# A hybrid state-space, attention and retrieval layer: part of the sorting, the state transposes and the value projection put at other places in the program

## The chip, the cores and the metric

The kernel runs on one core of a Trainium2 chip. The metric is device time of one execution in microseconds (us). Before the change, three timed runs gave 998.7 us as their median (997.2 to 999.82). TensorE multiplies (PE in the profile, its weight loads PEld), VectorE is DVE, ScalarE is ACT, GpSimd is POOL, SyncE (SP) issues the DMAs.

## The reference

One decoder layer over 256 tokens of 1024 numbers. Cut to what matters here:

```
proj = h @ w_in                                  # u | q | k | v, 512 columns each
y_ssm = _s5(u, ...)                              # 32 groups of a diagonal complex state, scan, GELU, GLU
y_att = _moba(q, k, v)                           # 8 heads of 64, causal over one block of 256
h = _layernorm(DN_ALPHA * h + concat([y_ssm, y_att]) @ w_out, ...)
# then the retrieval, per token:
q = (h @ w_q).reshape(tokens, 8 heads, 2, 128)
s = einsum('thcd,hcnd->thcn', q, sub_keys)       # 16 score lists of 128 for a token
s1, i1 = top_k(s[:, :, 0], 16); s2, i2 = top_k(s[:, :, 1], 16)
cand = s1[..., :, None] + s2[..., None, :]       # best 16 of them: eidx, softmax g
out = einsum(g * gelu(h . expert_u[eidx]), expert_v[eidx])
```

## The kernel before, in words

Almost all products are made of float32 matrices split into a high and a low part: ScalarE casts `hi`, VectorE (sometimes GpSimd) subtracts to get `lo`, and TensorE runs three passes (xh times hi, xl times hi, xh times lo). The retrieval is computed densely: all 16384 expert rows are streamed through and the gates are multiplied in.

A scheduler fixes one order of instructions for each engine when the program is built. It works from the order in which the code is written and from what depends on what; `tc.issue_after(x)` keeps what a block issues on x's engine behind x. On the chip each engine follows its list, so an instruction that waits holds all that stands behind it.

**The mixer** is written as steps named in `CFG['order']`, run by `do(w)`. The steps that matter: `u`, `q`, `k`, `v` are the four projections (`tokproj`, line 162, and `chproj`, line 173; 16 or 32 products each, and each float32 product is two MATMULs in the trace). `b` makes the state matrix `Bbd` on VectorE. `min` (`s5_min`, line 346) transposes it on TensorE in 32 products, and ScalarE copies them to `MinT`. `e0` and `e1` (line 410) multiply U by MinT, 64 columns wide. `s0`, `s1` are the scans on VectorE. `a0` and `a1` are four attention steps each (`attend`): scores of two heads (line 517: 64 rows, 128 columns, and line 521, the mask), row maximum on VectorE, exponential on ScalarE, transposes of the result (line 531). `kin` (line 392), `p0`, `p1`, `o0`, `o1` and `glu` close the mixer.

PSUM banks come from three pools: `w` with four (pw in the trace), `s` with two (psb), `a` with two (pa). `e0` takes both banks of `s`, `e1` both of `a`; the value projection uses `s`, the transposed probabilities use `a`.

**The routing**: `w_q` comes as 16 matrices `hc`. The first four are done together; hc = 4 to 15 are loaded and split one by one (line 826 and 828; with hc % 4 == 3 the subtraction is on GpSimd) and multiplied by `dense`. `scores(hc, ..)` makes for each of the two token halves b one list of 128 scores (line 812, 813), 32 lists in all, and while hc < EARLY (16 before) `top16` sorts it at once on VectorE: MAX, MAX_INDEX, MATCH_REPLACE, MAX, MAX_INDEX (lines 801 to 805). Three of these five are two instructions in the trace. The rest of the routing, `route(b)`, is a generator of steps; the main loop over 64 rows of `expert_u` (pairs, `u_pair`, u0 to u63; each `lo` is line 79) takes STEPS steps of it in its first PAIRS pairs. In `route(b)` ScalarE expands the indices `topi[b]` of all 16 lists of its half (`fv`, line 896).

Of the kernel before, what the change touches and what calls it, by code (L numbers as in the profile page):

```python
# [15 lines left out]
OP = mybir.AluOpType  # L16
# [25 lines left out]
def f32(ap):  # L42
    return ap.bitcast(F32)


CFG = dict(order='mask zero u par b min q rt rot k e0 e1 s0 a0 a0 a0 a0 s1 a1 a1 a1 a1 v c0 c kin p0 o0 p1 o1 glu',
           glu='VV',
           post='VV',
           yt='AAAAVVVVVVVPVVVV',
# [4 lines left out]
def layer(ctx, tc, I, out, tap=None, upto=None):  # L54
    nc = tc.nc
    V, S, P, PE = nc.vector, nc.scalar, nc.gpsimd, nc.tensor
# [45 lines left out]
    def sbank(shape):  # L102
        return ps.tile(shape, F32, tag="s", bufs=2, name="psb")
# [6 lines left out]
    with ExitStack() as px:  # L110
# [6 lines left out]
        with ExitStack() as mx:  # L117
# [5 lines left out]
            def eng(g, i):  # L123
                return P if CFG[g][i] == "P" else V

            prm = se.tile([128, 1088], F32, name="prm")
            xT = const.tile([128, ND, T], F32, tag="xh", name="xT")
# [25 lines left out]
            Uv = U.rearrange("p a b c -> p a (b c)")  # L153
            qk = sb.tile([128, 2, 4, T], F32, name="qk")

            def tokproj(blk, pt):
                for q in range(4):
                    w = w_in(blk, q)
                    for k in range(2):
                        d = 2 * q + k  # L160
                        for b in range(2):
                            PE.matmul(pt[b], xT[:, d, 128 * b:128 * b + 128],  # L162
                                      w[:, 512 * k:512 * k + 512], start=d == 0, stop=d == 7)

            def chproj(blk, scale):
                pt = [pbank([128, 2, T])[:, 0] for _ in range(4)]
                for q in range(4):
                    w = w_in(blk, q)
                    for k in range(2):
                        d = 2 * q + k  # L170
                        for m in range(4):
                            c = slice(512 * k + 128 * m, 512 * k + 128 * m + 128)
                            PE.matmul(pt[m], w[:, c], xT[:, d], start=d == 0, stop=d == 7)  # L173
                for m in range(4):
                    S.activation(qk[:, blk - 1, m], pt[m], AF.Copy, scale=scale)


            pw = sb.tile([128, 40, NPAIR], F32, name="pw")
# [117 lines left out]
            rot = sb.tile([128, 2, NPAIR, NCH], F32, name="rot")  # L296
# [44 lines left out]
            def s5_min():  # L341
                for ri in range(2):
                    for a in range(4):
                        pt = sbank([128, 4, 128])
                        for i in range(4):
                            PE.transpose(pt[:, i], Bbd[:, ri, 4 * a + i].rearrange("p j g -> p (j g)"),
                                         ident)
                        S.copy(MinT[:, ri, 4 * a:4 * a + 4], pt)
# [65 lines left out]
            def s5_scan(h, e, Sst):  # L414
# [13 lines left out]
                zr, zi = b4[1][:, sl], b4[3][:, sl]  # L428
                E = CFG["post"][h]
                V.tensor_tensor(b4[0][:, sl], zr, c_, op=OP.mult)  # L430
# [9 lines left out]
            def s5_out(h, Sst, yT):  # L440
# [10 lines left out]
                for j in range(4):  # L451
                    for q in range(4):
                        o, i = (yT[32 * q:32 * q + 32, 2 * h:2 * h + 2, :, j, :],
                                Y[32 * j:32 * j + 32, 2 * h:2 * h + 2, q])
                        e = CFG["yt"][4 * j + q]
                        S.copy(o, i) if e == "A" else (P if e == "P" else V).tensor_copy(o, i)
# [99 lines left out]
            M = {}  # L556
            zx = sb.tile([128, 2, NPAIR, NCH], F32, tag="zx", name="zx") if "P" in CFG["post"] else None

            def do(w):
                if w == "zero":  # L560
                    V.memset(Bbd, 0.0)
                    P.memset(Cbd, 0.0)
                    P.memset(Rt[:, :, 0:1], 0.0)
                    S.activation(Kin, ident[:, None, :].to_broadcast([128, NPAIR, 128]), AF.Copy,
                                 scale=0.0)
                elif w == "u":
                    pu = [abank([128, 512]) for _ in range(2)]
                    tokproj(0, pu)
                    for b in range(2):
                        V.transpose(U[:, :, b, :], pu[b].rearrange("p (a g) -> p a g", g=32))  # L570
                elif w == "q":
                    chproj(1, 0.125)
                elif w == "k":
                    chproj(2, 1.0)
                elif w == "v":
                    pv = [sbank([128, 512]) for _ in range(2)]
                    tokproj(3, pv)
                    M["v"] = vn = sb.tile([128, 2, 512], F32, tag="vn", name="vn")
                    for b in range(2):
                        S.copy(vn[:, b], pv[b])  # L580
                elif w == "par":
                    M["p"] = s5_params()
                elif w == "b":
                    s5_b(M["p"][0])
                elif w == "c0":
                    s5_c0()
                elif w == "c":
                    s5_c()
                elif w == "rt":
                    s5_rt(M["p"][1])  # L590
                elif w == "rot":
                    s5_rot()
                elif w == "min":
                    s5_min()
                elif w == "kin":
                    s5_kin()
                elif w in ("e0", "e1"):
                    M[w] = s5_e(int(w[1]))
                elif w in ("s0", "s1"):
                    if "S" not in M:  # L600
                        M["S"] = sb.tile([128, 2, NPAIR, NCH + 1], F32, tag="MinT", name="Sst")
                        P.memset(M["S"][:, :, :, 0:1], 0.0)
                    s5_scan(int(w[1]), M["e" + w[1]], M["S"])
                elif w in ("o0", "o1"):
                    if "y" not in M:
                        M["y"] = se.tile([128, 4, 2, 4, 32], F32, tag="yT", name="yT")
                    s5_out(int(w[1]), M["S"], M["y"])
                elif w == "mask":
                    masks()
                elif w in ("a0", "a1"):  # L610
                    if w not in M:
                        M[w] = attend(int(w[1]))
                    next(M[w])
                elif w in ("p0", "p1"):
                    values(int(w[1]), M["v"])
                elif w == "glu":
                    glu(M["y"])
                else:
                    raise ValueError(w)

            for w in CFG["order"].split():
                do(w)
# [14 lines left out]
            po = [[pbank([128, 512]) for _ in range(2)] for _ in range(2)]  # L637
            LATE = CFG["late"]
            W3 = sb.tile([128, 4, 1024], F32R, tag="MinT", name="W3")
# [79 lines left out]
            for q in range(4):  # L719
                raw = stream.tile([128, 1024], F32, tag="raw", bufs=RAWB, name="raw")  # L720
                for k in range(2):
                    c = 256 * q + 128 * k
# [3 lines left out]
                if q < 2:  # L726
                    r = late.tile([128, 2, 1024], F32R, tag="W4", bufs=2, name="W4")
                    hi, lo = r[:, 0], r[:, 1]
                else:
                    hi, lo = (stream.tile([128, 1024], F32R, tag=t, bufs=n, name=t)  # L730
                              for t, n in (("hi", HIB), ("lo", LOB)))
# [61 lines left out]
    with ExitStack() as rx:  # L793
# [10 lines left out]
            V.max(vals[:, 8:16], tmp)  # L804
            V.max_index(idx[:, 8:16], vals[:, 8:16], tmp)

        EARLY = 16

        def scores(hc, qT):
            for b in range(2):  # L810
# [7 lines left out]
        for hc in range(4, 16):  # L818
            raw = load(I["w_q"][hc])
            if hc == 4:  # L820
                with tc.issue_after(w4dma.ins):
                    nc.sync.dma_start(keys, I["keys"])
            hi, lo = (stream.tile([128, 1024], F32R, tag=t, bufs=n, name=t)
                      for t, n in (("hi", HIB), ("lo", LOB)))
            with tc.issue_after(cast.ins) if hc == 4 else ExitStack():
                S.copy(hi, raw)
            with tc.issue_after(normed.ins) if hc == 4 else ExitStack():
                (P if hc % 4 == 3 else V).tensor_tensor(lo, raw, f32(hi), op=OP.subtract)
            pt = abank([128, 2, T])[:, 0]
            dense(PE, pt, hi, lo, xh, xl)  # L830
            qT = sb.tile([128, T], F32, tag="qT", bufs=2, name="qT")
            S.copy(qT, pt)
            scores(*todo.pop(0))
            if len(todo) > 1:
                scores(*todo.pop(0))
            todo.append((hc, qT))
# [99 lines left out]


        steps, last = chain(route(0), route(1)), weigh()
        STEPS, PAIRS, GAP = 36, 26, 2
        done = 0  # L940
        for n in range(HALF // 2):
            low, ac = u_pair(2 * n)
# [25 lines left out]
    with tc.tile_pool(name="gk", bufs=1) as gk:  # L968
# [38 lines left out]
        for n in range(HALF // 2):  # L1007
# [3 lines left out]
            m = GT * made  # L1011
            made = due
            pt = sbank([128, 2, T])
            for r in range(2):
                hi, lo = split(load(I["u"][HALF + 2 * n + r]), P if r else V)
# [7 lines left out]
            raw = gk.tile([128, 2, T], F32, tag="ga", bufs=2, name="ga")  # L1023
# [5 lines left out]
        for i, t in enumerate(("o1", "o1", "eq")):  # L1029
            w = gk.tile([128, 2, T], F32R, tag=t, bufs=2 if t == "o1" else 1, name="wg")  # L1030
# [160 lines left out]
```

## Time and profile before

| | |
|---|---|
| median of 3 timed runs | 998.7 us (997.2 to 999.82) |
| the profiled execution: its own time, its span | 999.71 us, 997.9 us |
| PE busy | 965.8 us, 97% of the span |
| PEld, DVE busy | 855.0 us (86%), 714.9 us (72%) |
| ACT, POOL busy | 459.0 us (46%), 161.5 us (16%) |
| mean granted TensorE clock | 0.988 |
| chain that ended last | PE 81%, DVE 17%, issue 1% |

A busy share is an average over stages. TensorE is busy almost throughout; what it still waits for is read stage by stage, from the idle time ahead of its rows, and from the granted clock: 1.00 is full speed (2.4 GHz), 0.50 half of it (1.2 GHz), and at half speed TensorE counts as busy all the same.

### The profile page before, as it was taken

The numbers are of one execution on the slowest core, as the hardware profiler recorded it, in microseconds if no ns is written. First come the engines' busy times: TensorE is split into PE (matmuls) and PEld (weight loads), VectorE is DVE, ScalarE is ACT, GpSimd is POOL, SyncE is SP. The second block draws the span as 40 slices with busy tenths as digits, with TensorE's granted clock in tenths as the row PEclk, the third lists the DMA queues.
The fourth block names the chain that finished last, engine by engine and source line by source line (L and its number), as shares of the span: only waits on it lengthen the run. The fifth ranks groups of instructions, "written<-read, shape, count | busy, mean of one in ns | idle before, by whom it ended". The sixth has DMA issues, their size and how long they took to land.

```text
span 997.9 us, 16315 instructions
## 1 busy us (share of the span) xinstructions
PE 965.8 (97%) x6286; PEld 855.0 (86%) x6286; DVE 714.9 (72%) x1396; ACT 459.0 (46%) x737; POOL 161.5 (16%) x92
## 2 busy tenths in 40 slices
PE   7899999999999999999999999999999999999995
PEld 3785977989999999999999988888888888888884
DVE  8955477997766755988789999755555555555556
ACT  3224454545454445454444334544555454455552
POOL 2000003100000000354556565500000000000002
PEclk9889999999999999999999999999999999999998
DMA  8311284436555666355443434656566686666661
GB/s 326 117 43 43 82 256 134 143 126 194 186 186 177 188 185 178 124 151 154 143 151 123 130 125 148 212 184 195 190 193 190 197 274 198 193 190 193 191 198 51
DMA packets 49789, 166.24 MB, mean 167 GB/s; under 512 B 5296, under 2 KB 9392, under 8 KB 49584
## 3 DMA queue, kind: packets, MB, share of 16 engines
q1 hardware_dynamic: 49712, 165.20, 52.6%
q8 instruction: 49, 0.80, 0.3%
q14 instruction: 28, 0.23, 0.1%
HBM read 163.09 MB, written 2.10 MB: 166 GB/s over the span
## 4 chain that ended last, share of the span: by engine, by line
PE 81%; DVE 17%; issue 1%; ACT 0%; DVEq 0%
PE pw L1041 35%; PE psb L1111 29%; PE pa L1111 3%; PE pw L173 3%; DVE lo L72 2%; DVE o L984 2%; DVE act L996 2%; PE pw L989 2%; PE pw L646 2%; PE psb L162 2%; DVE o L981 1%; PE pw L517 1%; DVE eq L982 1%; PE pw L392 1%; PE psb L446 1%
## 5 line engine op out<-in xcount | busy, mean ns | idle before, releaser
L72 DVE TENSOR_TENSOR lo<-raw,hi 128x1024 fp32r<-128x1024 f32 x163 | 211.3, 1296 | 152.8 <-ACT hi L71 148.3
L71 ACT CAST hi<-raw 128x1024 fp32r<-128x1024 f32 x195 | 206.1, 1057 | 200.1 <-PE pw L1041 166.4
L1111 PE MATMUL psb<-xh,lo 128*128 128x256 f32 x1024 | 152.6, 289 | 6.5 <-DVE lo L79 4.3
L1111 PE MATMUL psb<-xh,hi 128*128 128x256 f32 x1024 | 158.1, 291 | 0.4 <-ACT act L848 0.4
L1111 PE MATMUL psb<-xl,hi 128*128 128x256 f32 x1024 | 153.7, 289 | 0.0
L1041 PE MATMUL pw<-hi,wh 128*128 128x512 f32 x492 | 151.9, 389 | 1.0 <-ACT wh L961 1.0
L1041 PE MATMUL pw<-hi,wl 128*128 128x512 f32 x492 | 152.1, 390 | 0.1
L1041 PE MATMUL pw<-lo,wh 128*128 128x512 f32 x492 | 151.8, 389 | 0.0
L1111 PEld LDWEIGHTS psb<-xh,lo 128*128 128x128 f32 x1024 | 133.9, 192 | 7.3 <-DVE lo L79 4.5
L1111 PEld LDWEIGHTS psb<-xh,hi 128*128 128x128 f32 x1024 | 135.5, 192 | 2.3 <-issue 1.0
L1111 PEld LDWEIGHTS psb<-xl,hi 128*128 128x128 f32 x1024 | 132.9, 191 | 0.0
L79 DVE TENSOR_TENSOR lo<-raw,hi 128x1024 fp32r<-128x1024 f32 x64 | 78.1, 1221 | 57.1 <-ACT hi L78 57.1
L72 POOL TENSOR_TENSOR lo<-raw,hi 128x1024 fp32r<-128x1024 f32 x32 | 83.0, 2592 | 218.0 <-ACT hi L71 202.5
L1041 PEld LDWEIGHTS pw<-hi,wh 128*128 128x128 f32 x492 | 92.3, 188 | 20.5 <-ACT wh L961 1.4
L1041 PEld LDWEIGHTS pw<-hi,wl 128*128 128x128 f32 x492 | 92.2, 188 | 20.1 <-DVE wl L962 1.0
L1041 PEld LDWEIGHTS pw<-lo,wh 128*128 128x128 f32 x492 | 92.4, 188 | 19.1
L78 ACT CAST hi<-raw 128x1024 fp32r<-128x1024 f32 x64 | 66.9, 1047 | 89.5 <-PE psb L1111 81.3
L996 DVE SCALAR_TENSOR_TENSOR act<-pw,act 128x256 f32<-128x256 f32 x124 | 66.0, 589 | 18.1 <-PE pw L989 18.1
L999 ACT ACTIVATE act<-pw 128x256 f32<-128x256 f32 (+29 forms) x64 | 27.8, 434 | 103.6 <-DVE act L996 81.5
L989 PE MATMUL pw<-o,o 128*128 128x128 f16 x512 | 73.0, 225 | 1.2 <-DVE o L984 1.0
L1025 POOL TENSOR_TENSOR act<-act,ga 128x512 f32<-128x512 f32 (+29 forms) x32 | 50.5, 1578 | 86.6 <-ACT ga L1024 59.1
L1084 POOL TENSOR_TENSOR tail<-tail 128x512 f32<-128x512 f32 x2 | 2.5, 1286 | 345.5 <-ACT tail L1083 345.5
(307 smaller groups left out, 1116.7 us busy)
## 6 DMA issues: line engine op xcount, KB each, us to landing
raw<-in_u SPq DMA_DIRECT2D x128, 512.0 KB, 3.6
raw<-in_v SPq DMA_DIRECT2D x128, 512.0 KB, 3.6
w<-in_w_in SPq DMA_DIRECT2D x15, 512.0 KB, 8.9
raw<-in_w_q SPq DMA_DIRECT2D x12, 512.0 KB, 3.9
raw<-in_w_out SPq DMA_DIRECT2D x8, 512.0 KB, 3.8
raw<-in_w_q SPq DMA_DIRECT2D x8, 256.0 KB, 4.1
xT<-in_xT SPq DMA_DIRECT2D x4, 256.0 KB, 5.0
raw<-in_w_glu SPq DMA_DIRECT2D x2, 512.0 KB, 4.0
```

The lines of the kernel that those rows point to most:

```text
L71: S.copy(hi, raw)
L72: eng.tensor_tensor(lo, raw, f32(hi), op=OP.subtract)
L78: S.copy(hi, raw)
L79: return hi, lo, V.tensor_tensor(lo, raw, f32(hi), op=OP.subtract)
L162: PE.matmul(pt[b], xT[:, d, 128 * b:128 * b + 128], w[:, 512 * k:512 * k + 512], start=d == 0, stop=d == 7)
L173: PE.matmul(pt[m], w[:, c], xT[:, d], start=d == 0, stop=d == 7)
L989: PE.matmul(pt[:, i], o1[:, (q + i) // 2, :, i % 2], o2[:, k, (q + i) // 2, :, i % 2], start=k == 0, stop=k == 1)
L996: V.scalar_tensor_tensor(a, pt[:, :, HALF * h:HALF * h + n], 1.0 / GSC, a, op0=OP.mult, op1=OP.mult)
L999: S.activation(act[1][:, done:, tq].rearrange("p i t -> p t i"), pt[:, :, HALF + done:], AF.Copy, scale=1.0 / GSC)
L1025: P.tensor_tensor(a[:, :, :m1], a[:, :, :m1], raw[:, :, :m1], op=OP.mult)
L1041: PE.matmul(acc[b][c], x[:, tk], w[:, 512 * c:512 * c + 512], start=first and j == 0, stop=last and j == 2)
L1111: PE.matmul(pt, w[:, 128 * d:128 * d + 128], x[:, d], start=n == 0 and d == 0, stop=n == 2 and d == ND - 1)
```

## The change

Four things. The transposes of `min` are kept behind the last product of the query projection. The value projection is cut: its first half (`va`) is written ahead of the attention steps, its second (`vb`) after them. EARLY goes from 16 to 12, so that the lists of hc = 12 to 15 (eight of the 32) are sorted in `route`, which gets 44 steps for the 36 it had, over the same 26 pairs. And the subtraction of hc = 7, 11 and 15 goes from GpSimd to VectorE.

```diff
-CFG = dict(order='mask zero u par b min q rt rot k e0 e1 s0 a0 a0 a0 a0 s1 a1 a1 a1 a1 v c0 c kin p0 o0 p1 o1 glu',
+CFG = dict(order='mask zero u par b q min rt rot k e0 e1 s0 va a0 a0 a0 a0 s1 a1 a1 a1 a1 vb c0 c kin p0 o0 p1 o1 glu',
...
-            def tokproj(blk, pt):
-                for q in range(4):
+            def tokproj(blk, pt, qs=range(4)):
+                for q in qs:
...
-                            PE.matmul(pt[m], w[:, c], xT[:, d], start=d == 0, stop=d == 7)
+                            mm = PE.matmul(pt[m], w[:, c], xT[:, d], start=d == 0, stop=d == 7)
...
+                return mm
...
-                    chproj(1, 0.125)
+                    M["q"] = chproj(1, 0.125)
...
-                elif w == "v":
-                    pv = [sbank([128, 512]) for _ in range(2)]
-                    tokproj(3, pv)
+                elif w == "va":
+
+                    pv = M["pv"] = [sbank([128, 512]) for _ in range(2)]
+                    tokproj(3, pv, range(2))
+                elif w == "vb":
+                    pv = M["pv"]
+                    tokproj(3, pv, range(2, 4))
...
-                    s5_min()
+                    with tc.issue_after(M["q"].ins):
+                        s5_min()
...
-        EARLY = 16
+        EARLY = 12
...
-                (P if hc % 4 == 3 else V).tensor_tensor(lo, raw, f32(hi), op=OP.subtract)
+                V.tensor_tensor(lo, raw, f32(hi), op=OP.subtract)
...
-        STEPS, PAIRS, GAP = 36, 26, 2
+        STEPS, PAIRS, GAP = 44, 26, 2
```

The orders of the engines show what moved. First TensorE, from the end of the u projection (pa<-w,xT) to `e0` (psb<-U,MinT); line 173 is the query and then the key projection, psb<-ident,Bbd are the state transposes. Before:

```order
L162 MATMUL pa<-w,xT 128x512 x12
L173 MATMUL pw<-xT,w 128x256 x8
L346 MATMUL psb<-ident,Bbd 128x128 x8
L173 MATMUL pw<-xT,w 128x256
L346 MATMUL psb<-ident,Bbd 128x128 x8
L173 MATMUL pw<-xT,w 128x256 x2
L346 MATMUL psb<-ident,Bbd 128x128 x8
L173 MATMUL pw<-xT,w 128x256
L346 MATMUL psb<-ident,Bbd 128x128 x8
L173 MATMUL pw<-xT,w 128x256 x52
L410 MATMUL psb<-U,MinT 128x64 x16
```

Of the change:

```order
L162 MATMUL pa<-w,xT 128x512 x12
L173 MATMUL pw<-xT,w 128x256 x32
L347 MATMUL psb<-ident,Bbd 128x128 x8
L173 MATMUL pw<-xT,w 128x256
L347 MATMUL psb<-ident,Bbd 128x128 x8
L173 MATMUL pw<-xT,w 128x256
L347 MATMUL psb<-ident,Bbd 128x128 x8
L173 MATMUL pw<-xT,w 128x256
L347 MATMUL psb<-ident,Bbd 128x128 x8
L173 MATMUL pw<-xT,w 128x256 x29
L411 MATMUL psb<-U,MinT 128x64 x16
```

The first transpose stood behind 8 products of the query projection and stands behind all 32 of them.

Next TensorE in the attention; psb<-w,xT is the value projection, pw<-qk and pw<-mb,identb a score and its mask. Before, from the last scores of `a0` into those of `a1` (two score products to a mask):

```order
L521 LDWEIGHTS identb
L521 MATMUL pw<-mb,identb 128x128
L517 MATMUL pw<-qk 128x128
L521 LDWEIGHTS identb
L521 MATMUL pw<-mb,identb 128x128
L162 MATMUL psb<-w,xT 128x512 x3
L517 MATMUL pw<-qk 128x128 x2
L521 LDWEIGHTS identb
L521 MATMUL pw<-mb,identb 128x128
L517 MATMUL pw<-qk 128x128 x2
L521 LDWEIGHTS identb
```

Of the change, from `e0` on:

```order
L411 MATMUL psb<-U,MinT 128x64 x16
L411 MATMUL pa<-U,MinT 128x64 x16
L162 MATMUL psb<-w,xT 128x512 x8
L518 MATMUL pw<-qk 128x128
L522 LDWEIGHTS identb
L522 MATMUL pw<-mb,identb 128x128
L518 MATMUL pw<-qk 128x128
L522 LDWEIGHTS identb
L522 MATMUL pw<-mb,identb 128x128
L518 MATMUL pw<-qk 128x128
L522 LDWEIGHTS identb
L522 MATMUL pw<-mb,identb 128x128
```

Eight of the 16 value products stand ahead of the scores now. The other eight come after all scores of `a0` and `a1`; before, three stood between the two and three more behind the first four of `a1`'s eight. All of `a0`'s and `a1`'s scores follow each other now, with only the eight transposes of `a0`'s probabilities among them, the first of these behind six and a half of `a0`'s eight score products.

Last VectorE where the sorting ends and the expert rows begin; both pieces end with the subtraction for the expert row u3. Before:

```order
L801 MAX tops<-sco 128x8
L804 MAX tops<-tmp 128x8
L802 MAX_INDEX topi<-tops,sco 128x8
L805 MAX_INDEX topi<-tops,tmp 128x8
L803 MATCH_REPLACE tmp<-tops,sco 128x128
L867 TENSOR_TENSOR cand<-tops 128x8x16
L804 MAX tops<-tmp 128x8
L867 TENSOR_TENSOR cand<-tops 128x8x24
L805 MAX_INDEX topi<-tops,tmp 128x8
L867 TENSOR_TENSOR cand<-tops 128x8x16
L867 TENSOR_TENSOR cand<-tops 128x8x8
L79 TENSOR_TENSOR lo<-raw,hi 128x1024
```

Of the change (the first subtraction here is u2's):

```order
L807 MAX tops<-sco 128x8
L808 MAX_INDEX topi<-tops,sco 128x8
L809 MATCH_REPLACE tmp<-tops,sco 128x128
L810 MAX tops<-tmp 128x8
L811 MAX_INDEX topi<-tops,tmp 128x8
L79 TENSOR_TENSOR lo<-raw,hi 128x1024
L807 MAX tops<-sco 128x8
L808 MAX_INDEX topi<-tops,sco 128x8
L809 MATCH_REPLACE tmp<-tops,sco 128x128
L810 MAX tops<-tmp 128x8
L811 MAX_INDEX topi<-tops,tmp 128x8
L79 TENSOR_TENSOR lo<-raw,hi 128x1024
```

Between u2's subtraction and u3's stood six lists and the first candidates; one list stands there now. Further up, the subtraction for hc = 8 stood behind four lists and stands behind ten; from there on two lists stand to each subtraction, as before, and hc = 12 follows hc = 11 without a list between.

## Rows read from the trace of the kernel before

**Rows 1.** Page, part 4: the chain that ended last, by engine.

```profile
PE 81%; DVE 17%; issue 1%; ACT 0%; DVEq 0%
```

**Rows 2.** Busy time of each engine (and instructions) in four stretches, then granted clock, DMA.

```profile
28.00:35.00 7.00, 5.49 (x21) 5.05 (x22) 6.89 (x17) 2.34 (x4) 0.00 (x0) 0.54 0.15 50
...
67.00:69.50 2.50, 2.50 (x16) 1.75 (x15) 2.50 (x4) 0.00 (x0) 0.15 (x1) 1.00 0.01 3
69.50:76.50 7.00, 7.00 (x18) 3.96 (x18) 6.53 (x14) 1.61 (x8) 0.00 (x0) 0.51 0.00 0
...
98.00:122.00 24.00, 24.00 (x215) 23.59 (x215) 11.56 (x29) 9.24 (x20) 0.28 (x1) 1.00 0.24 74
```

**Rows 3.** TensorE by time, projections: start, length, operation, count, idle before and its releaser.

```profile
22.53 3.62 PE L173 MATMUL pw<-xT,w 128*128 128x256 f32 x16
29.51 1.94 PE L346 MATMUL psb<-ident,Bbd 128*128 128x128 f32 x8 [3.37 <-DVE Bbd L320]
...
35.46 1.04 PE L346 MATMUL psb<-ident,Bbd 128*128 128x128 f32 x8
36.33 0.60 PE L173 MATMUL pw<-xT,w 128*128 128x256 f32 x2
...
37.72 22.61 PE L173 MATMUL pw<-xT,w 128*128 128x256 f32 x104
60.16 3.68 PE L410 MATMUL psb<-U,MinT 128*128 128x64 f32 x32
```

**Rows 4.** VectorE by time: the last part of Bbd, and the first scan product.

```profile
31.77 0.95 DVE L320 TENSOR_TENSOR Bbd<-big,big 64x768 f32<-64x768 f32 x1
...
62.10 0.69 DVE L418 TENSOR_TENSOR big<-psb,rot 128x512 f32<-128x512 f32 x1 [7.36 <-PE psb L410]
```

**Rows 5.** TensorE by time: scores of a0 and a1, and the value projection.

```profile
67.35 0.48 PE L517 MATMUL pw<-qk 64*128 64x128 f32 x2
...
69.71 0.79 PE L517 MATMUL pw<-qk 64*128 64x128 f32 x2
...
73.36 4.29 PE L162 MATMUL psb<-w,xT 128*128 128x512 f32 x6
77.58 0.71 PE L517 MATMUL pw<-qk 64*128 64x128 f32 x4
...
80.68 2.79 PE L162 MATMUL psb<-w,xT 128*128 128x512 f32 x6
```

**Rows 6.** TensorE by time: third pass of hc 8, of hc 9, and u2 to u4.

```profile
185.64 1.12 PE L1111 MATMUL pa<-xh,lo 128*128 128x256 f32 x8
...
188.96 1.12 PE L1111 MATMUL pa<-xh,lo 128*128 128x256 f32 x8
...
219.98 1.12 PE L1111 MATMUL psb<-xh,hi 128*128 128x256 f32 x8
220.94 1.12 PE L1111 MATMUL psb<-xl,hi 128*128 128x256 f32 x8
226.35 1.93 PE L1111 MATMUL psb<-xh,lo 128*128 128x256 f32 x8 [4.29 <-DVE lo L79]
...
230.81 1.12 PE L1111 MATMUL psb<-xh,lo 128*128 128x256 f32 x8
```

**Rows 7.** VectorE by time: first list, subtractions of hc 9, hc 10 and u3.

```profile
173.24 0.49 DVE L801 MAX8 tops<-sco 128x8 f32<-128x128 f32 x2 [0.81 <-ACT sco L813]
...
185.60 1.21 DVE L828 TENSOR_TENSOR lo<-raw,hi 128x1024 fp32r<-128x1024 f32 x1
...
189.08 1.43 DVE L828 TENSOR_TENSOR lo<-raw,hi 128x1024 fp32r<-128x1024 f32 x1
...
225.07 1.22 DVE L79 TENSOR_TENSOR lo<-raw,hi 128x1024 fp32r<-128x1024 f32 x1
```

**Rows 8.** GpSimd by time: the subtraction of hc 7.

```profile
172.84 2.39 POOL L828 TENSOR_TENSOR lo<-raw,hi 128x1024 fp32r<-128x1024 f32 x1 [14.82 <-PE pw L812]
```

**Rows 9.** ScalarE by time: the first expansion of indices.

```profile
221.35 1.90 ACT L896 CAST fv<-topi 128x2048 bf16<-128x2048 uint32 x1 [6.84 <-DVE topi L805]
```

## The prediction

> **What bounds the kernel now.** I read the page first: TensorE is busy for 97% of the span, and the chain that ended last runs through it for 81% [rows 1]. So a change gains only where TensorE idles or runs at the low clock; work moved between the other engines counts by what TensorE waits for. Next the busy times by stretch, with the granted clock [rows 2]. The clock is 0.54 from 28 to 35 us and 0.51 from 69.5 to 76.5 us, and in the second of these TensorE shows 7.00 of 7.00 us busy: half speed hides in the busy share. Last TensorE by time at three places, for idle time and who ended it: 3.37 us ahead of the state transposes, ended by VectorE's Bbd [rows 3]; no idle, but slow rows, in the scores of `a0` [rows 5]; and 4.29 us ahead of u3's third pass, ended by VectorE's `lo` [rows 6].
>
> **Part 1: transposes behind the query projection.** Before, TensorE does 16 MATMULs from 22.53 us, waits for Bbd, and resumes at 29.51 at the low clock. `e0` begins at 60.16. What the stretch from 22.53 needs without the wait and at full clock: 128 MATMULs of 128x256 at (60.16 - 37.72) / 104 = 0.216 us are 27.6 us; 32 transposes at (36.33 - 35.46) / 8 = 0.109 us are 3.5 us [rows 3]. That ends at 53.6, so 6.5 us go: the idle time and the half-speed rows behind it. The cover of the wait is the query projection itself: it now runs to 22.5 + 64 x 0.216 = 36.3 us, and the last part of Bbd is done at 32.7 [rows 4]. What is late next? VectorE's first scan product waited 7.36 us for `e0` [rows 4], so up to that much earlier it still follows TensorE. The bound is from 0 (were the query weights late) to 6.5; I take 6.5, since nothing in the stretch waits for a load now and the order of SyncE's loads stays; those that wait for the query's buffers come earlier.
>
> **Part 2: the value projection.** The same products run in another order; what changes is the clock and one wait.
>
> Before, the clock falls 2.4 us after `a0`'s narrow scores begin, at 69.7, although no idle stands there; four score products with their masks take 69.71 - 67.35 = 2.36 us at full and 73.36 - 69.71 = 3.65 us at half speed. It returns in the first six MATMULs of the value projection, which take 4.29 us against 2.79 later [rows 5]. So that spell cost 1.3 + 1.5 = 2.8 us.
>
> Now the first half of the value projection stands between `e1` and `a0`, and no wide product between `a0`'s first score and `a1`'s last. I take it that the clock falls as far into `a0` as before, and comes back only in wide products, as in both of these spells. Then the price is: half of `a0` 1.3 us as before; `a1`'s eight score products, 80.68 - 77.58 = 3.10 us for four at full speed [rows 5], so 6.2 us, longer by 3.65 / 2.36 = 1.55, or 3.4 us; eight transposes among them at 0.109 more each, 0.9 us; and six value MATMULs at 1.5 us as before. That is 7.1 us, against 2.8: 4.3 us more.
>
> The wait: the first transposed probabilities go to the bank of `e1`'s real part, whose last reader on VectorE now stands behind the third row maximum. That needs six score products, 6 x 0.59 = 3.5 us from `a0`'s start, and two VectorE operations of about half a microsecond each (the product beside it took 0.69 [rows 4]); TensorE is there after six and a half products, 3.8 us. That is 0.7 us of waiting. With the clock down after four products, 4 x 0.59 + 2 x 0.91 + 1.0 = 5.2 us stand against TensorE's 4.6: 0.6 us, which I take. Part 2 in sum: 4.9 us lost. Its bounds: from 2.1 us gained (no low spell, and the wait) to 16 us lost (the last rival).
>
> Here a page speaks for another result. The rows show the granted clock at 0.51 with TensorE busy throughout and 1.00 in the narrow products from 98 to 122 us [rows 2], so what decides in between is not idle time alone. The Trainium skill (TensorE: Matmul & The Clock Gate, section "Why this matters for your kernels") asks only that no long idle gaps stand between bursts of matmuls to keep the clock up. By that rule 0.7 us of waiting would not lower it, and the total would be the second rival's; the trace disagrees with it at 69.5 us.
>
> **Part 3: eight lists later, three subtractions to VectorE.** Before, VectorE works without idle from 173 us on, and u3's subtraction starts at 225.07 behind the lists [rows 7]. TensorE would have begun that pass 0.96 us after 220.94, at 221.90; it began at 226.35, and its next three groups took 230.81 - 226.35 = 4.46 us where 3 x 0.96 = 2.88 are due: the clock had fallen in the wait [rows 6]. Lost: 4.45 + 1.58 = 6.0 us.
>
> Now the walk down VectorE's queue. hc 7's subtraction starts when GpSimd's did, at 172.84 [rows 8], and takes 1.2 us: the first list starts at 174.0, not 173.24. Ten lists took 185.60 - 173.24 less one subtraction, 11.2 us [rows 7], and stand ahead of hc 8's subtraction now: it runs from 185.2 to 186.4, and TensorE wants it at 185.64 [rows 6]. That is 0.8 us of new waiting. Then a round of two lists and a subtraction is 189.08 - 185.60 = 3.48 us [rows 7] against TensorE's 188.96 - 185.64 = 3.32 us [rows 6], over three rounds to hc 11, 0.5 us more. hc 12's subtraction follows at once, and the queue is ahead again. From hc 11's at 195.6: 1.3 us to hc 12, four rounds to u0 (14 us), 1.4 us to u1, then twice one list and a subtraction (some 2.7 us, as a list alone has nothing to overlap with) to u3: about 218, where TensorE wants it at 221.9 + 1.3 = 223.2. The wait and the low clock go; 6.0 - 1.3 = 4.7 us gained. Between 0 and 6.0 this is near the upper end, since VectorE has 4 us in hand at u3.
>
> The eight lists go beside the expert rows: 11.2 / 10 = 1.1 us each, 9 us more on an engine that has two subtractions (2.4 us) and under two routing steps to do in the 6 x 0.96 = 5.8 us of a pair; I cost them at nothing there. ScalarE's `fv` now waits for hc 15's list behind u4's subtraction, and u5's cast stands behind it: by the walk `fv` starts near 223, the cast ends near 226, and TensorE wants u5 at 227. That is the tightest cover, 1 us.
>
> **Sum.** 999.7 - 6.5 + 4.9 - 4.7 = 993.4 us against the profiled execution, 1.0 us over the median of the runs. For the timed runs: 992.4 us.
>
> **Rivals.**
>
> 1. The low spell stays as short as before: `a1` alone brings the clock back. Its score products are denser than `a0`'s (0.78 us with two score MATMUL pairs and a mask, against 0.59 with one). Against it: no narrow products ended a spell in this trace. Then part 2 loses 0.6 us: 988.1.
> 2. No low spell, as the idle-gap rule has it: the wide half ahead of `a0` keeps the clock up. For it, the narrow products from 98 to 122 us at 1.00 [rows 2]; against it, `a0` without wide products at its end is longer than before. Part 2 gains 2.1 us: 985.4.
> 3. Sorting's stall only moves: `fv` holds ScalarE (it already waited 6.84 us there, unseen behind the lists [rows 9]), u5's cast is late, and TensorE idles and cools again. For it the 1 us of cover; against it, eight lists fewer ahead. Part 3 gains nothing: 997.1.
> 4. Slower: the low clock outlasts the second half of the value projection, as its products are mixed with transposes of `a1`, and holds through `kin`. Then the other ten value MATMULs cost (4.29 - 2.79) / 6 = 0.25 us more each, 2.5 us; 16 transposes 1.8 us; and `kin`'s 64, at 0.109 us more each like a transpose, 7.0 us. That is 11.3 more: 1003.7. It decides if the clock is still below 1.00 when the last three value products begin. Against it, the spell at 28 us ended among transposes and projections mixed [rows 3].
>
> **How the numbers follow.** Forecast 0.53 (own range 990 to 995), rival 1 0.17, rival 2 0.10, rival 3 0.12, rival 4 0.05, the rest 0.03. From rival 2 to just below rival 3 holds about 0.83: 984.5 to 996.5. What can be told from no change is 0.3%, 3.0 us: faster is below 995.7. The forecast, its two better rivals and few of rival 3 are faster, 0.82; most of rival 3 and the near part of rival 4 within, 0.12; slower 0.06.
>
> **What would show it.** Part 1: no idle ahead of the state transposes, clock 1.00 from 22 to 54 us, `e0` near 53.7. Part 2: score MATMULs of `a1` at the half-speed length, and `kin` starting about 1.6 us earlier than before; had they full length, rival 1 or 2 holds and `kin` starts 6 to 9 us earlier. Part 3: 0.8 us of idle ahead of hc 8's third pass, none ahead of u3's. The prediction is wrong if a wait of over 1 us stands anywhere between u0 and u10, or if the clock returns between `a0` and `a1`.

## The result, and the profile after

Six timed runs of the changed kernel have a median of 992.06 us (989.45 to 994.41), six of the kernel before 998.64 (997.2 to 1000.0): ratio 0.9935, 95% interval 0.9917 to 0.9953, 6.5 us faster. The forecast was 992.4. The profiled execution took 994.41 us (span 992.6) against 999.71 (997.9): 5.3 less, where the sum had 6.3 less (993.4). It was the slowest of the six.

| place in the trace | before | after | difference so far |
|---|---|---|---|
| `e0` begins | 60.16 | 53.59 | -6.57 |
| `kin` begins | 98.21 | 96.50 | -1.71 |
| first product of `glu` behind its wait | 127.63 | 125.94 | -1.69 |
| u3's third pass begins | 226.35 | 222.70 | -3.65 |
| u4's third pass begins | 230.81 | 225.58 | -5.23 |
| span | 997.9 | 992.6 | -5.3 |

The page's chain that ended last, by engine, after [rows 1]:

```profile
PE 85%; DVE 13%; issue 1%; ACT 0%; DMA 0%; SPq 0%; DVEq 0%; ACTq 0%
```

VectorE's share of the path fell by four points. The chain no longer runs through VectorE's work ahead of Bbd and of u3's `lo`, whose two waits are gone; the waits themselves were 7.7 us, under one point.

TensorE by time, after, over the projections (start, length, operation, count) [rows 3]:

```profile
22.31 13.98 PE L173 MATMUL pw<-xT,w 128*128 128x256 f32 x64
36.12 1.04 PE L347 MATMUL psb<-ident,Bbd 128*128 128x128 f32 x8
...
41.07 12.68 PE L173 MATMUL pw<-xT,w 128*128 128x256 f32 x58
53.59 3.68 PE L411 MATMUL psb<-U,MinT 128*128 128x64 f32 x32
```

No idle time stands ahead of the transposes, and they have their full-speed length. Stretches after (busy time and instructions of PE, PEld, DVE, ACT, POOL, then granted clock, DMA) [rows 2]:

```profile
22.00:54.00 32.00, 32.00 (x167) 27.84 (x165) 30.57 (x75) 9.85 (x22) 0.00 (x0) 1.00 0.34 112
...
73.00:90.00 17.00, 17.00 (x55) 10.96 (x55) 8.89 (x14) 5.71 (x24) 0.00 (x0) 0.50 0.01 1
98.00:122.00 24.00, 24.00 (x215) 23.60 (x213) 10.97 (x29) 10.33 (x20) 0.41 (x2) 1.00 0.25 69
```

The price is the second row: 17 us at half speed with TensorE 100% busy, where [rows 2] had 7. TensorE by time there [rows 5]:

```profile
67.70 0.48 PE L518 MATMUL pw<-qk 64*128 64x128 f32 x2
...
68.28 0.48 PE L518 MATMUL pw<-qk 64*128 64x128 f32 x2
...
71.58 0.33 PE L532 MATMUL pa<-ident,p 128*128 128x128 f32 x1
...
72.58 1.02 PE L518 MATMUL pw<-qk 64*128 64x128 f32 x4
...
73.97 0.79 PE L518 MATMUL pw<-qk 64*128 64x128 f32 x2
...
83.09 1.22 PE L518 MATMUL pw<-qk 64*128 64x128 f32 x4
...
84.47 1.22 PE L518 MATMUL pw<-qk 64*128 64x128 f32 x4
...
86.13 1.91 PE L162 MATMUL psb<-w,xT 128*128 128x512 f32 x2
...
90.59 1.02 PE L162 MATMUL psb<-w,xT 128*128 128x512 f32 x2
...
96.50 7.17 PE L393 MATMUL pw<-Cbd,Bbd 128*32 128x128 f32 x64
```

Two score MATMULs take 0.48 us and then 0.79; four in `a1` take 1.22, before 0.71. All of `a0`'s scores are done at full speed: `a1`'s begin at 72.58, and the clock falls there (1.00 to 72.5 us, 0.50 from 73). Two wide value MATMULs take 1.91 us at first and 1.02 once the clock is back. No idle row stands ahead of the first transposed probabilities (71.58), and VectorE's last read of `e1`'s real part begins behind them:

```profile
71.66 0.68 DVE L423 TENSOR_TENSOR big<-pa,rot 128x512 f32<-128x512 f32 x1
```

TensorE at hc 8 and hc 9, after (in brackets the idle time and who ended it) [rows 6]:

```profile
185.90 1.21 PE L1117 MATMUL pa<-xh,lo 128*128 128x256 f32 x8 [0.64 <-DVE lo L834]
...
189.38 1.21 PE L1117 MATMUL pa<-xh,lo 128*128 128x256 f32 x8
```

0.64 us wait at hc 8, then rounds of 3.48 us for the 3.32 before, up to hc 11. VectorE's subtraction of u3, behind the lists, now begins at 217.08 (225.07 before, [rows 7]):

```profile
217.08 1.21 DVE L79 TENSOR_TENSOR lo<-raw,hi 128x1024 fp32r<-128x1024 f32 x1
```

It is 4.4 us ahead of TensorE, which has no idle row between u0 and u10.

### The profile page after: what moved, and what is told of

It reads as the page before. It is cut to its first block, busy times and chain, and to the rows that moved or that the text cites. A ratio compares the mean times of both kernels' runs of the same rounds, so it can differ in the third digit from the quotient of the medians.

```text
span 992.6 us, 16314 instructions
## 1 busy us (share of the span) xinstructions
PE 967.7 (97%) x6286; PEld 855.5 (86%) x6286; DVE 716.4 (72%) x1399; ACT 459.1 (46%) x737; POOL 154.4 (16%) x89
## 4 chain that ended last, share of the span: by engine, by line
PE 85%; DVE 13%; issue 1%; ACT 0%; DMA 0%; SPq 0%; DVEq 0%; ACTq 0%
PE pw L1047 35%; PE psb L1117 30%; PE pw L173 3%; PE pa L1117 2%; DVE lo L72 2%; DVE o L990 2%; PE pw L995 2%; DVE act L1002 2%; PE pa L162 2%; PE pw L652 2%; PE psb L162 2%; DVE o L987 1%; PE pw L518 1%; DVE eq L988 1%; PE pw L393 1%
```

## The experiments

In each run the kernel before was timed on the same chip (medians 994.9 to 997.7 us there), so ratios are compared, and a difference in us is the ratio's on 998.6. In brackets stand 95% intervals; 0.001 is 1 us. The code cuts are shortened.

**One part at a time.** Part 1 alone, from the changed kernel:

```diff
-order='... s0 va a0 a0 a0 a0 s1 a1 a1 a1 a1 vb c0 ...'
+order='... s0 a0 a0 a0 a0 s1 a1 a1 a1 a1 va vb c0 ...'
-EARLY = 12  (44 steps, subtractions on V)
+EARLY = 16  (36 steps, hc % 4 == 3 on P)
```

> The kernel before with part 1 alone: the state transposes behind the query projection; value projection, lists and subtractions as before. Theory (the three parts add up as the terms say): the wait for Bbd and the low clock behind it go, 6.5 us, so 992.1 us against 998.6; no idle time ahead of the first transpose, e0 near 53.7 us, kin 6.5 us earlier, so near 91.7 us. Rival (the low clock only moves): the spell saved at 28 us is given back in the attention, which now follows a longer stretch at full clock: the spell in a0 lasts as long as in the changed kernel (17 us) although the value projection is undivided; then 4 to 6 us come back and the time is 996 to 998 us, with kin later than 95 us.

993.03 us, ratio 0.9943 [0.9927, 0.9959]: 5.7 us gained. `e0` and `kin` come 7.0 and 6.9 us earlier (`kin` at 91.36), and the low spell in `a0` is no longer than before (from 63.3 to 70.1 us). The rival falls.

Part 3 alone:

```diff
-with tc.issue_after(M["q"].ins): s5_min()      (b q min)
+s5_min()                                       (b min q)
-order='... s0 va a0 ... a1 vb c0 ...'
+order='... s0 a0 ... a1 va vb c0 ...'
```

> The kernel before with part 3 alone: EARLY 12, 44 routing steps, the subtraction of hc 7, 11 and 15 on VectorE; mixer as before. Theory: the wait at u3 (4.45 us) and its cold clock (1.6 us) go, 0.6 to 1.3 us come new at hc 8 to 11: 4.7 to 5.4 us gained, 993.2 to 994.0 us against 998.6; between the third pass of hc 8 and u10 no wait over 0.3 us. Rival (sorting's stall only moves to a later pair, or the chip cools there all the same): 997 to 998.6 us.

994.32 us, ratio 0.9962 [0.995, 0.9974]: 3.8 us, less than the 4.7 to 5.4 expected, though 4.7 lies in the interval (2.6 to 5.0). The trace has 0.64 us at hc 8 and no wait at u3. It also has `kin` 2.3 us earlier than before, in a mixer that was not changed. Its stretches behind the Bbd wait:

```profile
24.00:28.00 4.00, 1.72 (x8) 1.16 (x7) 4.00 (x9) 0.00 (x0) 0.00 (x0) 1.00 0.90 307
28.00:32.00 4.00, 2.47 (x19) 2.22 (x20) 3.92 (x12) 1.55 (x3) 0.00 (x0) 1.00 0.14 58
32.00:36.00 4.00, 3.95 (x26) 3.17 (x26) 3.96 (x8) 2.75 (x6) 0.00 (x0) 1.00 0.02 4
```

The wait is there (3.8 us), the low clock behind it (0.54 from 28 to 35 us in [rows 2]) is not. So that spell, part of the 6.5 us of part 1, isn't in every execution.

Part 2 alone:

```diff
-with tc.issue_after(M["q"].ins): s5_min()      (b q min)
+s5_min()                                       (b min q)
-EARLY = 12  (44 steps, subtractions on V)
+EARLY = 16  (36 steps, hc % 4 == 3 on P)
```

> The kernel before with part 2 alone: the first half of the value projection ahead of a0, the second behind a1; transposes, lists and subtractions as before. Theory (narrow products without a wide one keep the clock low): a low spell of 15 to 18 us that begins in a0 and ends in the second half of the value projection, 4.3 to 4.9 us lost at kin, and perhaps the 1.2 us that the changed kernel lost at 127 us as well: 1002.9 to 1004.7 us against 998.6. Rival A (the long spell belongs to part 1, to the long stretch at full clock ahead of it): spell as before near 7 us, 998 to 999 us. Rival B (the value half ahead of a0 keeps the clock up, as its later fall in the changed kernel, 5.2 us into a0 for 2.4, suggests): no or a shorter spell, 996 to 998 us.

1003.93 us, ratio 1.0047 [1.003, 1.0065]: 4.7 us lost. The clock is low from about 78 to 95.7 us:

```profile
78.00:84.00 6.00, 6.00 (x23) 4.05 (x23) 4.79 (x7) 2.32 (x12) 0.00 (x0) 0.52 0.00 1
84.00:90.00 6.00, 6.00 (x22) 4.01 (x22) 2.68 (x5) 2.27 (x10) 0.00 (x0) 0.50 0.01 3
90.00:96.00 6.00, 6.00 (x20) 3.71 (x21) 1.79 (x3) 1.56 (x6) 0.00 (x0) 0.56 0.00 0
```

The theory holds and both rivals fall: the long spell belongs to part 2. The three parts alone add to -5.7 - 3.8 + 4.7 = -4.8 us, just within the interval of the whole (-8.3 to -4.7).

The change without part 2:

```diff
-order='... s0 va a0 a0 a0 a0 s1 a1 a1 a1 a1 vb c0 ...'
+order='... s0 a0 a0 a0 a0 s1 a1 a1 a1 a1 va vb c0 ...'
```

> The changed kernel without part 2: the value projection undivided at its old place, parts 1 and 3 kept. Theory (part 2 alone lengthens the spell): the low spell in a0 lasts about 7 us again, a1's score products take 0.71 us or less in place of 1.22, kin starts near 91.7 us in place of 96.5, so 4.3 to 4.8 us less: 987.3 to 987.8 us, and 986.1 if the new low spell at 127 us goes with it; faster than both kernels. Rival (the long spell comes with part 1, whatever the value projection does): 991 to 993 us, with a1's scores at 1.2 us.

989.91 us, ratio 0.9906 [0.9889, 0.9924]: 9.4 us under the kernel before, and 2.9 under the changed one, less than the 4.3 to 4.8 expected (its interval and the changed kernel's overlap a little). In the profiled execution, the slowest of the five, the spell lasted 10 us in place of 7, and `kin` began at 93.16, not at 91.7:

```profile
62.40:72.40 10.00, 10.00 (x23) 4.80 (x22) 9.22 (x18) 1.62 (x8) 0.00 (x0) 0.50 0.00 0
```

The new low spell at 125 us (below) stayed too. Parts 1 and 3 alone add to 9.5 us: nothing shows that they touch each other.

**What lets the clock fall.** The score products use 64 rows of the array; transposes, `kin` and the rest use 128. So the rows were changed alone:

```diff
-r = slice(64 * (n % 2), 64 * (n % 2) + 64)
+r = slice(0, 128)
```

> The changed kernel with every score product taken over all 128 rows of query and key in place of the 64 of one head (the scores of two heads are added, so this computes something else; the number, the columns and the length of the products stay, 0.24 us each at full clock). Theory (half the rows of the array is what lets the clock fall in the attention): no low spell between 67 and 90 us, a1's four score products take 0.71 us where they took 1.22, kin starts 7 to 8.5 us earlier, near 88 to 89.5, and the time is 983.5 to 985 us against 992.1. Rival (the rows don't matter; it is the short products themselves, or what came ahead): spell of about 17 us as before, 991.5 to 992.5 us.

981.45 us, ratio 0.9837 [0.9814, 0.9861]. TensorE by time:

```profile
68.20 0.44 PE L518 MATMUL pw<-qk 128*128 128x128 f32 x2
68.53 0.44 PE L518 MATMUL pw<-qk 128*128 128x128 f32 x2
...
74.84 0.66 PE L518 MATMUL pw<-qk 128*128 128x128 f32 x4
...
85.00 7.17 PE L393 MATMUL pw<-Cbd,Bbd 128*32 128x128 f32 x64
```

The clock is 1.00 from 20 to 112 us. More came than expected, `kin` 11.5 us earlier than in the changed kernel: two score MATMULs and a mask take 0.33 us where they took 0.58, so the "0.24 us each" of the expectation was no length of a product. With the mask over 128 rows between products of 64, 0.245 us of each step went with the change between 64 and 128 rows, and it counted as busy. Both lengths are from rows at full clock, so this part of the gain has nothing to do with the clock.

> The same edit on the kernel without part 2 (value projection undivided at its old place, parts 1 and 3 kept; 989.9 us). Theory (rows): no spell, so the place of the value projection no longer matters: kin near 88 us in place of 93.2, 984 to 985.5 us, the same as the run with the divided value projection within 1 us. Rival (rows don't matter): spell of 7 to 10 us as before, 989 to 990.5 us.

The same row edit on the kernel without part 2 gave 982.57 us, ratio 0.9836 [0.981, 0.9862], `kin` at 84.65: without a spell the place of the value projection makes no difference.

That edit changed two things, the rows of the products and the time lost in the changes, which I call gaps. To part them, score products of 64 rows without a mask between them:

```diff
-PE.matmul(o, q[64 rows], k[64 rows], start=True, stop=kb != b)
-if kb == b: PE.matmul(o, identb, mb, start=False, stop=True)
+for z in range(4): PE.matmul(o, q[64 rows], k[64 rows], start=z == 0, stop=z == 3)
```

> The changed kernel with each score product over 64 rows issued four times into the same sum, and without the mask products (so no mask, and four times the scores): long stretches of 64-row products with no 128-row product between them but the transposes. Theory S (what costs is each change between a 64-row and a 128-row product, a gap of 0.245 us that counts as busy, and these gaps let the clock fall): a MATMUL takes 0.11 us, the clock stays at 1.00 in a0 and a1 although both last longer (7 and 14 us in place of 4.6 and 6.4), kin before 100 us, time 990 to 996 us. Theory R (half the rows is what lets the clock fall): 0.50 from some 3 to 6 us into a0 until the second half of the value projection, a MATMUL at 0.2 us, kin after 108 us, time over 1002 us.

1017.85 us (one time; it has four times the scores and no mask). TensorE by time, and stretches:

```profile
67.72 3.05 PE L519 MATMUL pw<-qk 64*128 64x128 f32 x28
...
77.70 2.51 PE L519 MATMUL pw<-qk 64*128 64x128 f32 x14
```

```profile
74.00:76.00 2.00, 2.00 (x14) 1.64 (x14) 1.81 (x4) 1.25 (x7) 0.00 (x0) 1.00 0.00 0
76.00:78.00 2.00, 2.00 (x9) 1.21 (x9) 1.55 (x2) 0.25 (x2) 0.00 (x0) 0.56 0.08 18
78.00:110.00 32.00, 32.00 (x146) 27.72 (x144) 3.90 (x7) 6.17 (x21) 0.00 (x0) 0.50 0.06 17
```

A MATMUL of 64 rows takes 3.05 / 28 = 0.11 us, as over 128, so the gaps are gone but at the transposes; the clock falls all the same (one idle time, 0.40 us at 73.5, stands 2.5 us ahead of the fall), stays at 0.50 for the 34 us up to the wide products that begin at 110.1, and comes back in these, at 113.6. Theory R holds: products over half the rows went with the low clock here, gaps or not. The other half, gaps between products over 128 rows, was not tested.

The wide products spread among the scores:

```diff
-order='... s0 va a0 a0 a0 a0 s1 a1 a1 a1 a1 vb c0 ...'
+order='... s0 a0 v0 a0 a0 v1 a0 s1 a1 v2 a1 a1 v3 a1 c0 ...'
```

> The changed kernel with the value projection in four quarters, one behind the first and third step of a0 and of a1, so that wide products stand within every four steps of narrow ones. Theory (the clock stays low for as long as only narrow products follow, and wide ones bring it back): if it falls, it returns in the next quarter; spell at most 7 us, kin between 90 and 93.5 us, 986 to 989.5 us. Rival (score products keep the clock down wherever the wide ones stand): spells of 10 us or more in sum, kin after 94.5 us, 990 to 993 us.

987.4 us, ratio 0.9902 [0.9876, 0.9929], 3.3 under the changed kernel (here too the intervals overlap a little). The clock is 1.00 throughout the attention, better than the 7 us allowed:

```profile
66.00:72.00 6.00, 6.00 (x23) 3.06 (x22) 3.94 (x8) 0.81 (x4) 0.00 (x0) 1.00 0.00 0
72.00:78.00 6.00, 6.00 (x28) 3.55 (x29) 5.07 (x8) 2.90 (x12) 0.00 (x0) 1.00 0.28 87
78.00:84.00 6.00, 6.00 (x30) 3.62 (x29) 4.95 (x8) 3.81 (x11) 0.00 (x0) 1.00 0.30 91
```

So a value projection that is cut has to stand in four pieces among the scores, not in two around them. It does not beat the undivided one, though: the kernel without part 2 has 0.9906, the same within the noise.

**The subtractions.** On the kernel without part 2:

```diff
-V.tensor_tensor(lo, raw, f32(hi), op=OP.subtract)
+(P if hc % 4 == 3 else V).tensor_tensor(lo, raw, f32(hi), op=OP.subtract)
```

> The kernel without part 2, and the subtractions of hc 7, 11 and 15 on GpSimd again, as before the change; EARLY 12 and 44 steps kept. Theory (the 0.6 us wait at hc 8's third pass is hc 7's subtraction standing ahead of the ten lists on VectorE): no wait over 0.2 us at hc 8, 9 or 10, rounds of 3.32 us from hc 8 on, 0.6 to 1.2 us less than the kernel without part 2, which can't be told from no change by one time, but by the rows. Rival (the lists alone are too many): the wait at hc 8 stays at 0.5 us or more.

The wait at hc 8 is gone and the rounds are 3.32 us, as the theory had it (TensorE shows no idle row from 170 to 200 us). Its one time, 983.78 us, was 6 us under the kernel with VectorE's, too much for that. It was timed again:

> The kernel with GpSimd's three subtractions again, timed in rounds, since its one look came out 6 us under the kernel with VectorE's. Theory A (the rows of that look: 1.1 us at hc 8 to 11, 2.2 us of later waits on VectorE's subtraction gone): 985 to 987 us against 989.9. Theory B (the look was a lucky execution, with a shorter low spell in a0 and none at 125 us; only the 1.1 us are due to the edit): 988 to 989.5 us.

986.49 us, which lies in A's range; but the kernel before took 994.9 us on this chip, and the ratio, 0.9903 [0.9884, 0.9923], is that of the kernel with VectorE's subtractions (0.9906). On 998.6 it is 988.9, in B's range, with A's upper end at the edge of the interval (987.0 to 990.9): one time of one execution, without the ratio, would have misled.

**A version from it.** Parts 1 and 3, GpSimd's subtractions, and every query head with zeros in the other 64 rows. The room is that of the transposed probabilities of `a1`, whose part n is written when the scores of step n are done:

```diff
+P.memset(pTs[1], 0.0)
...
-S.activation(qk[:, 0, m], pt[m], AF.Copy, scale=0.125)
+for g in range(2):
+    r = slice(64 * g, 64 * g + 64)
+    S.activation(pTs[1][r, 2 * (m // 2) + g, m % 2], pt[m][r], AF.Copy, scale=0.125)
...
-PE.matmul(o, qk[r, 0, h // 2, 128 * b:128 * b + 128], qk[r, 1, h // 2, ...])
+PE.matmul(o, pTs[1][:, n, i, 128 * b:128 * b + 128], qk[:, 1, h // 2, ...])
```

> The same computation as the reference, with parts 1 and 3 but the value projection undivided and the subtractions of hc 7, 11 and 15 on GpSimd; and the query written twice, each head's 64 rows with zeros in the other 64, so that every score product runs over 128 rows of query and key and still gives one head's scores. Theory (the rows that a product covers decide, whatever is in them): no low spell, score and mask take 0.33 us in a0 in place of 0.58, as with the summed heads; kin near 85 us, and with the wait at hc 8 gone 978 to 982 us: faster than every kernel so far. Rival (rows of zeros don't keep the clock up): the products are as short, but a low spell of 7 us or more stands in a0, and the time is 983 to 986 us.

979.73 us, ratio 0.9844 [0.9822, 0.9866]: 15.6 us under the kernel before, 9 under the changed one. By the ratio, on 998.6, that is 983.0, outside the theory's range (978 to 982) and at the edge of the rival's (983 to 986), since the kernel before took 994.9 on this chip; the rows decide between them. Score and mask take 0.33 us, and there is no low spell, neither in `a0` nor behind `glu`'s waits: rows of zeros do as well as others.

```profile
61.27 0.44 PE L523 MATMUL pw<-qk,pT 128*128 128x128 f32 x2
61.60 0.44 PE L523 MATMUL pw<-qk,pT 128*128 128x128 f32 x2
...
85.25 7.17 PE L398 MATMUL pw<-Cbd,Bbd 128*32 128x128 f32 x64
```

```profile
60.00:66.00 6.00, 6.00 (x42) 4.84 (x42) 6.00 (x10) 1.62 (x8) 0.16 (x1) 1.00 0.00 1
66.00:72.00 6.00, 6.00 (x31) 3.87 (x30) 6.00 (x11) 0.22 (x1) 0.00 (x0) 1.00 0.00 1
```

The same rows of the kernel with GpSimd's subtractions, the one that this version was made from:

```profile
60.46 0.48 PE L518 MATMUL pw<-qk 64*128 64x128 f32 x2
...
90.04 7.17 PE L393 MATMUL pw<-Cbd,Bbd 128*32 128x128 f32 x64
```

From `a0`'s first score to `kin` it takes 29.58 us, with the zeros 23.98: 5.6 us less. Most of it is not the clock: 16 steps of scores and mask at 0.245 us less each are 3.9 us, and the spell in that execution lasted 3.4 us (from 65.3 to 68.7), of which half speed costs 1.7.

## Why the prediction was right, point by point

- **Part 1: right.** 6.5 us in the sum, 6.57 at `e0`, no idle, clock 1.00. Timed alone it is 5.7 (4.1 to 7.3); the low spell that the profiled execution before held, and others lack, may be the difference, which was not shown.
- **Part 2: right in mechanism and in sum, the sum in part by luck.** 4.9 us in the sum, 6.57 - 1.71 = 4.86 in the trace, 4.7 timed alone. Two pieces did not come. The 0.6 us of waiting for the bank: the first transposed probabilities are written from 71.58 on, ahead of the last read of `e1`'s real part (71.66 to 72.34), so they have another bank than the step took. And the 1.3 us of `a0`: the clock fell 5.1 us after the first score, where the step took 2.4, when `a0`'s scores were over. One piece was sized too small: a product of `a1` with its mask took 1.38 us (83.09 to 84.47) for 0.78, which is up to 4.8 us for the eight where the step has 3.4. The step took its factor 1.55 from `a0`. The clock came back at 89.9, in the fourth value MATMUL, with transposes slow among them.
- **That the clock comes back only in wide products: borne out** in the trace of after, in the run of part 2 alone, and behind the 34 us of 64-row products. Wide products there were also products over 128 rows; which of the two counts for the return was not tested.
- **Part 3: right.** 0.64 us at hc 8 for 0.8, three rounds longer by 0.16, u3's subtraction done at 218.3 for 218. From 185.64 - (185.90 - 0.64) = 0.38 us ahead at hc 8, TensorE is 0.81 behind at hc 12 (199.73 against 188.96 + 3 x 3.32) and 5.23 ahead at u4: 1.2 lost and 6.0 gained, as the sum has it. Timed alone, 3.8 of 4.7.
- **Not foreseen:** behind the two waits of `glu`, the same in both kernels (1.0 and 0.6 us), the clock now fell at 127.5 us for 3.4 us; the lead went from 1.69 to 0.54 us. This is the 1 us by which the profiled execution missed the sum. That the median of the timed runs still came out at the forecast is luck: the profiled execution stood 2.35 us over it, where the forecast had allowed 1.0.
- **Rivals.** 1 and 2 (988.1 and 985.4) fell: the spell was longer. By the rule of the Trainium skill that drops come from idle gaps between bursts (TensorE: Matmul & The Clock Gate, section "Why this matters for your kernels") there was to be none; the trace disagrees, with 17 us at 0.50 and no idle row. 3 fell: `fv` begins at 220.22, u5's cast ends at 225.81, and TensorE wants it at 226.54, 0.7 us of cover for the 1 us expected. 4 fell: the clock was back before the last six value MATMULs.

## What to carry to other kernels

Read the granted clock beside the busy share, and where it falls without idle time, ask how many rows the products cover: heads of 64 padded with zeros to 128 rows were worth 6 us here (ratio 0.9844 with them, 0.9903 without), in the traces more by the changes of rows that went than by the clock. Where products over half the rows stay, don't put two halves of the wide ones around them: four pieces among them (0.9902) or the projection undivided (0.9906) were better than that (0.9935). And time a part alone before keeping it: the change was 6.5 us faster with a part in it that cost 3 to 5.

## What the runs showed that was not expected

- Changing between a 64-row and a 128-row product costs time that counts as busy: 0.58 us for two score MATMULs and a mask, 0.33 with all three over 128 rows.
- How long the clock stays low differs between executions. With the value projection undivided, the spell at `a0` lasted 6.8 us in four profiled executions, 10.2 in the run without part 2 and 3.4 in one of the two with GpSimd's subtractions. And the same waits are followed by a low clock in some executions only: behind the 3.4 to 3.8 us wait for Bbd about 7 us at half speed in the kernel before, half as long in the run of part 2 alone, none in that of part 3 alone; behind `glu`'s waits in 8 of the 13 profiled executions. What decides it was not tested.
- Two profiled executions of the kernel with GpSimd's subtractions differ by 2.2 us of span (982.0 and 984.2), and one lacks the two waits for VectorE's `lo` (2.2 us in sum) that the other twelve profiled executions have (at 597.9 and 613.8 us in the kernel before). Below stand the subtraction ahead of the first such wait in the run without part 2, and the one at the same place in the execution that lacks it, on VectorE, each with GpSimd's instruction beside it:

```profile
585.35 2.83 POOL L72 TENSOR_TENSOR lo<-raw,hi 128x1024 fp32r<-128x1024 f32 x1
...
585.86 3.40 DVE L72 TENSOR_TENSOR lo<-raw,hi 128x1024 fp32r<-128x1024 f32 x1
```

```profile
581.98 1.22 DVE L72 TENSOR_TENSOR lo<-raw,hi 128x1024 fp32r<-128x1024 f32 x1
...
582.13 2.68 POOL L1031 TENSOR_TENSOR act<-act,ga 128x448 f32<-128x448 f32 x1 [2.11 <-DVE o L990]
```

What tells them apart is who began first. VectorE's slow one began while GpSimd was in a subtraction of its own, and ended 1.08 us after that one; its fast one began 0.15 us ahead of GpSimd's product. In the 13 traces, from 380 to 660 us, some 80 such subtractions of VectorE's (rows of one) began while GpSimd was in an instruction and took 1.3 to 3.4 us, and some 480 began with GpSimd idle and took 1.2. Why the two engines did not meet in that one execution stays open.
